# A streaming-encoder layer on one core: sigmoid's difference in one VectorE instruction, operand splits moved from GpSimd to VectorE, the final norm woven into later MLP pairs, and another place for the residual tile

## The chip, the core and the metric

The kernel runs on 1 core of one Trainium2 chip. The core has TensorE (PE in the profile; its weight loads are PEld), VectorE (DVE), ScalarE (ACT), GpSimd (POOL) and SyncE (SP, which here issues every DMA). The metric is the device time of one execution in microseconds (us); lower is better. The kernel before takes 3223.38 us, the median of 3 runs (3223.03 to 3224.46).

## The reference, cut to what matters

One layer with 1024 features over 2048 prompt rows and 32 sample rows: attention, an output projection, an MLP, a gate, a final norm. All is fp32. What the change touches begins after the attention:

```python
h = h + merge(oa, ob, ...)                       # [oa, ob] @ w_out
c = rmsnorm(h, g_mlp)
h = h + jnp.square(jax.nn.relu(c @ w_up)) @ w_down
h = h + jax.nn.sigmoid(h @ w_ple_gate) * (p @ w_ple_proj)
y = rmsnorm(h, g_final)
```

## The kernel before

The rows lie in four blocks: three of 512 rows and one of 544 (the last 512 prompt rows and the 32 sample rows). After the attention everything is kept transposed, features on the 128 partitions and rows along the free axis, so a block's residual `h` is a tile of 128 x 8 x 512 (or 544).

Every matmul is done three times to get fp32 precision (`mm3`, L215 to L217): both operands are split into a high and a low part, and high x high, high x low and low x high are added up in PSUM. So each operand costs a split: ScalarE copies the high part (L180), and the low part is a subtraction, on GpSimd through `pool_tt` (L165 and L175) or on VectorE (L186). Weights are split too, right after their DMA (`wunit`; tiles `wr` for the raw weight, `piece` for the parts).

`pool_tt` cuts an operation into equal instructions of at most `PW` = 256 columns: 512 columns are two of 256, 272 columns two of 136, 544 columns three of 181 or 182.

The last stage does, in this order of the program:

- `gate(1)` and `final(1)` for block 1; its residual lies in the pool `hq`, the split operands of its gate in `actq`, the output rows in `uq`.
- New pools are opened. `wp4` holds weights, `uh` (20 buffers) and `wk4` (among others 8 buffers `tmp`) the temporaries, and `hh` (2 buffers) the residual of the blocks still to come. Pools are stacked from the left and from the right end of SBUF; a tile that comes to lie on older tiles waits until those are no longer used. `hh` is opened on the left, so it lies where `actq` was.
- `outproj(2)` and `outproj(3)`, with `oload(3)` woven in: the output projections of blocks 2 and 3 (PSUM tile `ops`).
- `gate(0)`, woven with `cparts(2)`; then `mlp7(2)`; `gate(2)`, woven with `cparts(3)`; `mlp7(3)`; `gate(3)` and `final(3)`.

`gate(b)` computes, for each of 8 groups `d` of 128 features, the product `gps` = h @ w_ple_gate and `pps` = p @ w_ple_proj. Sigmoid comes as exp(min(z,0) - ln(1 + exp(-|z|))): ScalarE does Abs, Exp, Ln (L1236, L1238, L1239), VectorE min(z,0) from PSUM into `sm` (L1237), GpSimd the difference (`sig<-sm,sig`, L165), ScalarE Exp (L1245), VectorE the product with `pps` (L1259), GpSimd adds it to h (`h<-h,sig`). For the last two `d` of block 3 VectorE does both GpSimd steps.

`cparts(b)` prepares the up-projection's operands for `mlp7`, which replaces 8 block products by 7 (a Strassen-like scheme): for each of 4 steps `k` it loads two groups of h from DRAM, scales them (L976), forms sums (L988 to L991), and splits seven operands into `cs` tiles, four low parts on GpSimd and three on VectorE.

`mlp7(b)` runs over 16 pairs of feature blocks. Each pair loads and splits its weights (L1163 to L1166 form weight sums), does 7 up products (`ups`, combined at L1135), squares (L1139, L1140), splits, and lets the down products (`dps`, added to h at L1124) of the pair before run in between. `next(m)` issues one pair.

`final(b)` is, for each 128 rows: transposes on TensorE (`yp`, L1281), a copy to SBUF (L1289), a sum of squares on ScalarE (L1291), a small rsqrt, two scalings (L1310), and two DMAs out. Transposes use the PSUM pool `mm` with 2 banks; up products take turns over one ring of `mm` and twice `md` (6 banks). `weave(m, f, 1)` issues one step of `f` after each step of `m`.

The program's order is a priority only: a planner with its own cost model of the engines writes out each engine's queue from it, taking what is ready by that model. On the chip each queue then runs in that order; an instruction that waits holds up all behind it on its engine. That holds for SP's queue of DMAs too.

Of the kernel before, what the change touches and what calls it, by code (L numbers as in the profile page):

```python
# [12 lines left out]
F32 = mybir.dt.float32  # L13
F32R = mybir.dt.float32r
AF = mybir.ActivationFunctionType
ALU = mybir.AluOpType
# [3 lines left out]
P = 128  # L20
# [13 lines left out]
BLK = 544  # L34
# [42 lines left out]
JB = [(0, 1), (2, 3), (4, 5), (6, 7, 8)]  # L77
ONP = (28, 1, 6)
ONQ = (8, 1, 1)
PW = 256  # L80


def drain(gen):
    for _ in gen:
        pass
# [13 lines left out]
def weave(main, side, step, i=0, n=1):  # L99
    for _ in main:  # L100
        if i % step == 0:
            for _ in range(n):
                next(side, None)
        i += 1
    drain(side)
# [37 lines left out]
class Kern:  # L143
# [14 lines left out]
    def pool_tt(self, out, a, b, op):  # L158
        nc = self.nc
        if len(out.shape) == 2:  # L160
            n = out.shape[1]
            m = -(-n // PW)
            for i in range(m):
# [3 lines left out]
        k, n = out.shape[1:]  # L167
        if n > PW:
            for i in range(k):
                self.pool_tt(out[:, i], a[:, i], b[:, i], op)  # L170
            return
        s = PW // n
        for i in range(0, k, s):
# [789 lines left out]
    def cparts(self, b, wk, cs, out, r):  # L963
        nc = self.nc
        n, t0 = BN[b], 512 * b
        m = n // 2
        names = ("b11", "b21", "t2", "t1", "t3", "b22", "t4")
        ops = {x: [cs.tile([P, 4, 272], F32R, tag="cs", name="cs")[:, :, :m] for _ in range(2)] for x in names}
        out[b] = ops
        for k in range(4):  # L970
            c = []
            for i in range(2):
                tmp = wk.tile([P, BLK], F32, tag="tmp", bufs=self.nt, name="tmp")[:, :n]
                kk = k + 4 * i
                self.dma(tmp, self.hS[:, kk, t0 : t0 + n])
                nc.vector.scalar_tensor_tensor(  # L976
                    tmp, tmp, self.g_mlp[:, kk : kk + 1], r, op0=ALU.mult, op1=ALU.mult
                )
                c.append((tmp[:, :m], tmp[:, m:]))
            (b11, b12), (b21, b22) = c  # L980
            raw = {"b11": b11, "b21": b21, "b22": b22, "t3": b22, "t1": b12, "t2": b11, "t4": b21}

            def parts(*which):
                for x, e in which:
                    self.split(ops[x][0][:, k], ops[x][1][:, k], raw[x], "act", e)

            parts(("b11", "pool"), ("b21", "dve"), ("b22", "pool"))
            nc.vector.tensor_tensor(b22, b22, b12, op=ALU.subtract)  # L988
            nc.vector.tensor_tensor(b12, b12, b11, op=ALU.subtract)
            nc.vector.tensor_tensor(b11, b22, b11, op=ALU.add)  # L990
            nc.vector.tensor_tensor(b21, b21, b11, op=ALU.subtract)  # L991
            parts(("t2", "dve"), ("t1", "pool"), ("t3", "dve"), ("t4", "pool"))
            yield

    def colnorm(self, *args):
# [203 lines left out]
    def gate(self, b, h, up, act, md, wk=None):  # L1199
        nc, a = self.nc, self.a  # L1200
        n, t0 = BN[b], 512 * b
        Wg, Wp = a["w_ple_gate"][0], a["w_ple_proj"][0]
        pT = [[up.tile([P, BLK], F32R, tag="u", name="pT") for _ in range(2)] for _ in range(2)]
        for i in range(2):
            for k in range(2):
                self.dma(pT[i][k][:, :n], self.pS[:, i, k, t0 : t0 + n])
        if wk is None and act.aw is None:
            hc = [act.tile([P, 4, 272], F32R, tag="cs", name="hc").rearrange("p a b -> p (a b)") for _ in range(8)]
            hH, hL = [[hc[4 * i + k // 2][:, BLK * (k % 2) : BLK * (k % 2) + n] for k in range(8)] for i in range(2)]
        elif wk is None:  # L1210
            hH = act.tile([P, 8, act.aw], F32R, tag="act", name="hH")
            hL = act.tile([P, 8, act.aw], F32R, tag="act", name="hL")
            hH, hL = [[t[:, k, :n] for k in range(8)] for t in (hH, hL)]
        else:
            hH, hL = [[up.tile([P, BLK], F32R, tag="u", name="hu")[:, :n] for k in range(8)] for _ in range(2)]
        for k in range(8):
            self.split(hH[k], hL[k], h[:, k, :n], "act", "dve" if k % 2 else "pool")
        for dq in range(2):
            ph, pl = self.wunit(
                Wp[:, 512 * dq : 512 * dq + 512].rearrange("(k p) c -> p k c", p=P), [2, 512]  # L1220
            )
            for d4 in range(4):
                d = 4 * dq + d4
                wh, wl = self.wunit(Wg[:, P * d : P * d + P].rearrange("(k p) c -> p k c", p=P), [8, P])
                for s0, sn in SUBS[b]:
                    pg = md.tile([P, 512], F32, tag="mm", name="gps")[:, :sn]
                    self.mm3(
                        pg,
                        [(wh[:, k], wl[:, k], hH[k][:, s0 : s0 + sn], hL[k][:, s0 : s0 + sn]) for k in range(8)],
                    )  # L1230
                    sg, sm = [
                        (up.tile([P, BLK], F32, tag="u", name=x) if wk is None
                         else wk.tile([P, BLK], F32, tag="tmp", bufs=self.nt, name=x))[:, :sn]
                        for x in ("sig", "sm")
                    ]
                    nc.scalar.activation(sg, pg, AF.Abs)  # L1236
                    nc.vector.tensor_scalar(sm, pg, 0.0, None, op0=ALU.min)  # L1237
                    nc.scalar.activation(sg, sg, AF.Exp, scale=-1.0)  # L1238
                    nc.scalar.activation(sg, sg, AF.Ln, bias=1.0)  # L1239
                    end = b == 3 and d >= 6  # L1240
                    if end:
                        nc.vector.tensor_tensor(sg, sm, sg, op=ALU.subtract)
                    else:
                        self.pool_tt(sg, sm, sg, ALU.subtract)
                    nc.scalar.activation(sg, sg, AF.Exp)  # L1245
                    pq = md.tile([P, 512], F32, tag="mm", name="pps")[:, :sn]
                    self.mm3(
                        pq,
                        [
                            (  # L1250
                                ph[:, k, P * d4 : P * d4 + P],
                                pl[:, k, P * d4 : P * d4 + P],
                                pT[0][k][:, s0 : s0 + sn],
                                pT[1][k][:, s0 : s0 + sn],
                            )
                            for k in range(2)
                        ],
                    )
                    nc.vector.tensor_tensor(sg, sg, pq, op=ALU.mult)  # L1259
                    hv = h[:, d, s0 : s0 + sn]  # L1260
                    if end:
                        nc.vector.tensor_tensor(hv, hv, sg, op=ALU.add)
                    else:
                        self.pool_tt(hv, hv, sg, ALU.add)
                yield
# [64 lines left out]
    def run(self):  # L1330
        tc, nc, a = self.tc, self.nc, self.a
        with ExitStack() as top:

            def opened(stack, name, bufs, space=None, side="left"):
                kw = {} if space is None else {"space": space}
                return stack.enter_context(
                    tc.tile_pool(name=name, bufs=bufs, side=side, reuse_waits="tile", **kw)
                )
# [16 lines left out]
            sg = opened(s12, "sg", 2)  # L1355
# [26 lines left out]
            with ExitStack() as x:  # L1382
                wk = opened(x, "setup", 1, side="right")
# [6 lines left out]
            with ExitStack() as x:  # L1390
                pool = opened(x, "a0", 1, side="right")
# [44 lines left out]
            with ExitStack() as x:  # L1436
                pool = opened(x, "a1", 1, side="right")
# [3 lines left out]
            wk = opened(sq_, "wk", 1)  # L1441
# [15 lines left out]
            up = Sized(opened(top, "uh", 20, side="right"), BLK)  # L1457
# [8 lines left out]
            for b in HALVES[0]:  # L1466
# [5 lines left out]
                m = self.mlp((b,), {b: (h,) + cn[b]}, wk, uq, mm, mm)  # L1472
# [16 lines left out]
            wk = opened(top, "wk4", 1, side="right")  # L1489
# [1 line left out]
            self.nt = 8  # L1491
            self.rawp = Rings((self.wp, "wr"), (wk, "wr"))
            self.gfin(fk)
            hh = opened(top, "hh", 2)
            with ExitStack() as x:
                act = Sized(opened(x, "acth", 2), BLK, True)
                weave(self.outproj(2, wk, oa[2], md, acc[2]), self.oload(3, wk, act, oa), 1, 0, OW)
# [11 lines left out]
            f = self.final(0, h, up, fk, mm)  # L1509
            h = hload(hh, BLK, 2)  # L1510
            m = self.mlp7(2, h, ops[2], wk, up, mm, md)
            next(m)
            drain(f)
            drain(m)
            g = self.gate(2, h, up, None, md, wk)
            next(g)
            weave(g, self.cparts(3, wk, cs, ops, r3), 1)
            f = self.final(2, h, up, fk, mm)
            h = hload(hh, BLK, 3)
            m = self.mlp7(3, h, ops[3], wk, up, mm, md)  # L1520
            next(m)
            drain(f)
            drain(m)
            g = self.gate(3, h, up, cs, md)
            f = self.final(3, h, up, fk, mm, md)
            for _ in range(5):
# [48 lines left out]
```

## Time and profile before

| what | us |
|---|---|
| median of 3 runs | 3223.38 (3223.03 to 3224.46) |
| the profiled execution: time, span from first to last instruction | 3225.84, 3224.0 |
| PE busy in the span | 3036.1 (94%) |
| PEld, DVE, ACT, POOL busy | 2691.8, 1854.1, 1885.7, 1959.8 |
| mean granted TensorE clock | 0.976 of full speed |
| `gate(1)`'s last product to `outproj(2)`'s first | 2159.5 to 2169.7 |
| `gate(0)` with `cparts(2)`, start of `mlp7(2)` | about 2272 to 2400 |
| steady part of `mlp7(2)` | 2400 to 2690 |
| `gate(2)` with `cparts(3)`, start of `mlp7(3)` | about 2695 to 2840 |

The times in the table's lower half are us from the span's start. PE is the engine that is busy nearly always, so what matters is where it is not: in the second half of the span these are a few short places at the seams between the stages above. The profile tells for each how long PE was idle and what it waited for; the busy time of the others in the same stretch tells what was late.

### The profile page before, as it was taken

The numbers are of one execution on the slowest core, as the hardware profiler recorded it, in microseconds if no ns is written. First come the engines' busy times: TensorE is split into PE (matmuls) and PEld (weight loads), VectorE is DVE, ScalarE is ACT, GpSimd is POOL, SyncE is SP. The second block draws the span as 40 slices with busy tenths as digits, with TensorE's granted clock in tenths as the row PEclk, the third lists the DMA queues.
The fourth block names the chain that finished last, engine by engine and source line by source line (L and its number), as shares of the span: only waits on it lengthen the run. The fifth ranks groups of instructions, "written<-read, shape, count | busy, mean of one in ns | idle before, by whom it ended". The sixth has DMA issues, their size and how long they took to land.

```text
span 3224.0 us, 53645 instructions
## 1 busy us (share of the span) xinstructions
PE 3036.1 (94%) x18265; PEld 2691.8 (83%) x18265; DVE 1854.1 (58%) x4436; ACT 1885.7 (58%) x4166; POOL 1959.8 (61%) x2782
## 2 busy tenths in 40 slices
PE   8998989999999999999999999999989999799998
PEld 7787777899987787878788788878778898699998
DVE  5156774544465554676756656535676665766663
ACT  6256775766675664766666656444555545545455
POOL 4466556433345444665555545678977778877675
PEclk9998999999999999999999999999999999899999
DMA  8787768976787645555563543538443334233231
GB/s 264 244 246 216 202 193 249 252 222 194 216 247 218 193 131 140 160 153 140 162 187 114 142 117 106 175 114 247 119 139 99 99 104 127 80 104 96 92 116 55
DMA packets 512506, 521.63 MB, mean 162 GB/s; under 512 B 37948, under 2 KB 393600, under 8 KB 512232
## 3 DMA queue, kind: packets, MB, share of 16 engines
q1 hardware_dynamic: 512232, 518.19, 54.8%
q8 instruction: 145, 2.38, 0.3%
q14 instruction: 129, 1.06, 0.1%
HBM read 412.08 MB, written 109.95 MB: 162 GB/s over the span
## 4 chain that ended last, share of the span: by engine, by line
PE 53%; DMA 4%; DVE 4%; POOL 2%; ACT 2%; issue 1%; SPq 0%; DVEq 0%; ACTq 0%; POOLq 0%
PE dps L215 7%; PE dps L216 7%; PE dps L217 7%; PE ups L215 6%; PE ups L216 6%; PE ups L217 6%; PE s L632 2%; PE gps L216 1%; PE gps L215 1%; PE gps L217 1%; PE tpp L704 1%; DMA wr<-w_up 1%; DMA tmp<-hS 1%; POOL piece L175 1%; PE ops L215 1%
## 5 line engine op out<-in xcount | busy, mean ns | idle before, releaser
L175 POOL TENSOR_TENSOR wl<-wr,wh 128x256 fp32r<-128x256 f32 x648 | 473.7, 762 | 328.9 <-ACT wh L180 318.4
L180 ACT ACTIVATE piece<-wr 128x512 fp32r<-128x512 f32 x412 | 254.0, 627 | 310.8 <-PE ups L216 160.5
L175 POOL TENSOR_TENSOR piece<-wr,piece 128x256 fp32r<-128x256 f32 x416 | 334.3, 828 | 119.2 <-ACT piece L180 106.4
L180 ACT ACTIVATE wh<-wr 128x1024 fp32r<-128x1024 f32 x228 | 240.8, 1057 | 196.9 <-PE qps L216 52.2
L165 POOL TENSOR_TENSOR wl<-wr,wh 128x256 fp32r<-128x256 f32 x264 | 198.8, 783 | 182.1 <-ACT wh L180 176.8
L215 PE MATMUL ups<-cs,piece 128*128 128x256 f32 (+1 forms) x896 | 256.9, 287 | 10.3 <-ACT cs L180 5.4
L215 PE MATMUL dps<-uh,piece 128*128 128x272 f32 (+1 forms) x768 | 247.1, 327 | 16.0 <-ACT uh L180 15.6
L217 PE MATMUL ups<-cs,piece 128*128 128x256 f32 (+1 forms) x896 | 256.7, 287 | 0.6 <-POOL piece L175 0.6
L216 PE MATMUL ups<-cs,piece 128*128 128x256 f32 (+1 forms) x896 | 256.0, 286 | 0.5 <-DVE cs L186 0.5
L1124 DVE TENSOR_TENSOR h<-h,dps 128x272 f32<-128x272 f32 (+1 forms) x384 | 191.1, 514 | 100.3 <-PE dps L217 99.8
L216 PE MATMUL dps<-ul,piece 128*128 128x272 f32 (+1 forms) x768 | 247.9, 324 | 0.4 <-DVE ul L186 0.4
L217 PE MATMUL dps<-uh,piece 128*128 128x272 f32 (+1 forms) x768 | 247.2, 324 | 0.0
L215 PE MATMUL qps<-aH,wh 128*128 128x512 f32 (+1 forms) x640 | 230.2, 360 | 5.9 <-DVE ql L475 4.1
L165 POOL TENSOR_TENSOR piece<-wr,piece 128x256 fp32r<-128x256 f32 x280 | 223.1, 830 | 15.6 <-ACT piece L180 15.1
L215 PE MATMUL dps<-uh,wh 128*128 128x512 f32 x512 | 209.9, 410 | 21.3 <-ACT wh L180 7.4
L216 PE MATMUL qps<-aL,wh 128*128 128x512 f32 (+1 forms) x640 | 228.8, 357 | 0.0
L217 PE MATMUL qps<-aH,wl 128*128 128x512 f32 (+1 forms) x640 | 228.3, 357 | 0.0
L1083 DVE TENSOR_TENSOR h<-h,dps 128x512 f32<-128x512 f32 x256 | 174.2, 682 | 83.2 <-PE dps L217 78.5
L632 PE MATMUL s<-ka,q 128*128 128x512 f32 (+3 forms) x768 | 187.7, 347 | 22.5 <-DMA ka<-kS 12.1
L215 PE MATMUL ups<-cH,wh 128*128 128x512 f32 x512 | 202.7, 396 | 0.5 <-DVE h L1083 0.4
L216 PE MATMUL dps<-ul,wh 128*128 128x512 f32 x512 | 202.7, 396 | 0.0
L217 PE MATMUL dps<-uh,wl 128*128 128x512 f32 x512 | 202.3, 395 | 0.0
(300 smaller groups left out, 9839.0 us busy)
## 6 DMA issues: line engine op xcount, KB each, us to landing
wr<-w_up SPq DMA_DIRECT2D x128, 512.0 KB, 4.1
wr<-w_down SPq DMA_DIRECT2D x128, 512.0 KB, 3.7
wr<-w_in SPq DMA_DIRECT2D x74, 512.0 KB, 4.6
q<-qS SPq DMA_DIRECT2D x128, 256.0 KB, 5.3
v<-vSa SPq DMA_DIRECT2D x64, 512.0 KB, 3.7
ka<-kS SPq DMA_DIRECT2D x32, 512.0 KB, 7.9
wr<-w_out SPq DMA_DIRECT2D x32, 512.0 KB, 5.3
wr<-w_ple_gate SPq DMA_DIRECT2D x32, 512.0 KB, 4.1
```

What stands on the lines that cost most here:

```text
L165: nc.gpsimd.tensor_tensor(out[:, sl], a[:, sl], b[:, sl], op=op)
L175: nc.gpsimd.tensor_tensor(out[:, sl], a[:, sl], b[:, sl], op=op)
L180: nc.scalar.activation(hi, raw, AF.Copy)
L215: nc.tensor.matmul(ps, lh, rh, start=start and i == 0, stop=False)
L216: nc.tensor.matmul(ps, lh, rl, start=False, stop=False)
L217: nc.tensor.matmul(ps, ll, rh, start=False, stop=stop and i == n - 1)
L632: nc.tensor.matmul(s, q[:, m, hl, P * qi : P * qi + nr], kt[:, m, k0 - kb : k0 - kb + n], start=hl == 0, stop=hl == 1)
L704: nc.tensor.transpose(tp[:kn, x, :nr], w[:nr, P * i : P * i + kn], self.ident[:nr, :nr])
L1083: nc.vector.tensor_tensor(hv, hv, ps, op=ALU.add)
L1124: nc.vector.tensor_tensor(hv, hv, ps, op=ALU.add)
```

## The change

`PW` becomes 272. In `cparts` two of the four low parts move from GpSimd to VectorE. In `gate` one VectorE instruction, min(z,0) - sig, read from PSUM and SBUF, replaces VectorE's min and GpSimd's difference; it comes after Ln, and the tile `sm` is gone. `hh` is opened on the right side of SBUF. After `gate(0)` and `gate(2)` two MLP pairs are issued ahead of the final norm instead of one, and then one tile of 128 rows of it after each further pair instead of all four at once.

```diff
-PW = 256
+PW = 272
@@ cparts
-            parts(("b11", "pool"), ("b21", "dve"), ("b22", "pool"))
+            parts(("b11", "pool"), ("b21", "dve"), ("b22", "dve"))
...
-            parts(("t2", "dve"), ("t1", "pool"), ("t3", "dve"), ("t4", "pool"))
+            parts(("t2", "dve"), ("t1", "dve"), ("t3", "dve"), ("t4", "pool"))
@@ gate
-                    sg, sm = [
-                        (up.tile([P, BLK], F32, tag="u", name=x) if wk is None
-                         else wk.tile([P, BLK], F32, tag="tmp", bufs=self.nt, name=x))[:, :sn]
-                        for x in ("sig", "sm")
-                    ]
+                    sg = (
+                        up.tile([P, BLK], F32, tag="u", name="sig") if wk is None
+                        else wk.tile([P, BLK], F32, tag="tmp", bufs=self.nt, name="sig")
+                    )[:, :sn]
                     nc.scalar.activation(sg, pg, AF.Abs)
-                    nc.vector.tensor_scalar(sm, pg, 0.0, None, op0=ALU.min)
                     nc.scalar.activation(sg, sg, AF.Exp, scale=-1.0)
                     nc.scalar.activation(sg, sg, AF.Ln, bias=1.0)
                     end = b == 3 and d >= 6
-                    if end:
-                        nc.vector.tensor_tensor(sg, sm, sg, op=ALU.subtract)
-                    else:
-                        self.pool_tt(sg, sm, sg, ALU.subtract)
+                    nc.vector.scalar_tensor_tensor(sg, pg, 0.0, sg, op0=ALU.min, op1=ALU.subtract)
                     nc.scalar.activation(sg, sg, AF.Exp)
@@ run
-            hh = opened(top, "hh", 2)
+            hh = opened(top, "hh", 2, side="right")
...
             m = self.mlp7(2, h, ops[2], wk, up, mm, md)
-            next(m)
-            drain(f)
-            drain(m)
+            for _ in range(2):
+                next(m)
+            weave(m, f, 1)
...
             m = self.mlp7(3, h, ops[3], wk, up, mm, md)
-            next(m)
-            drain(f)
-            drain(m)
+            for _ in range(2):
+                next(m)
+            weave(m, f, 1)
```

## The prediction

> **What bounds the kernel now.** I read the page's busy shares and its 40 slices first, then the stages by windows, then what PE waited for in each, then what the other engines did there.
>
> ```profile
> span 3224.0 us, 53645 instructions
> ...
> PE 3036.1 (94%) x18265; PEld 2691.8 (83%) x18265; DVE 1854.1 (58%) x4436; ACT 1885.7 (58%) x4166; POOL 1959.8 (61%) x2782
> ...
> PE   8998989999999999999999999999989999799998
> ...
> POOL 4466556433345444665555545678977778877675
> PEclk9998999999999999999999999999999999899999
> ```
>
> PE is the bound almost everywhere: 94%. In the last third it dips in slices 27, 30 and 35, which are the seams that the change touches, and there POOL, not PE, stands at 7 to 9. The windows give the seams in us:
>
> ```profile
> core 0: us, PE busy (x) PEld busy (x) DVE busy (x) ACT busy (x) POOL busy (x), PEclk, DMA share, GB/s
> 2150.00:2180.00 30.00, 23.35 (x99) 18.44 (x98) 14.14 (x24) 14.22 (x35) 19.78 (x28) 0.83 0.53 165
> 2210.00:2240.00 30.00, 24.69 (x158) 22.09 (x157) 15.80 (x20) 16.17 (x30) 25.90 (x32) 1.00 0.79 243
> 2276.00:2360.00 84.00, 70.24 (x348) 58.22 (x347) 66.33 (x82) 50.65 (x105) 80.03 (x93) 0.95 0.30 89
> 2318.00:2345.00 27.00, 20.59 (x110) 17.24 (x109) 25.67 (x31) 15.93 (x34) 27.00 (x30) 0.94 0.13 34
> 2345.00:2372.00 27.00, 19.65 (x120) 17.66 (x118) 15.95 (x24) 13.12 (x29) 25.29 (x33) 0.81 0.35 114
> 2372.00:2400.00 28.00, 24.01 (x159) 21.17 (x158) 24.76 (x51) 14.56 (x38) 18.45 (x22) 1.00 0.65 231
> 2694.00:2792.00 98.00, 74.94 (x365) 62.50 (x364) 66.68 (x81) 51.18 (x103) 92.18 (x123) 0.89 0.31 91
> 2748.00:2770.00 22.00, 9.74 (x48) 7.95 (x47) 20.62 (x24) 11.61 (x25) 18.37 (x26) 0.69 0.15 47
> 2770.00:2795.00 25.00, 14.21 (x97) 13.76 (x98) 12.86 (x20) 11.77 (x24) 24.82 (x33) 0.80 0.28 86
> ```
>
> PE's idle time is the window less its busy time. Seam A (end of `gate(1)`): 6.65. Seam B (start of `outproj(3)`): 5.31. Seam C (`gate(0)` into `mlp7(2)`): 6.41 + 7.35 + 3.99 = 17.75. Seam D (`gate(2)` into `mlp7(3)`): 12.26 + 10.79 = 23.05. Together 52.8. On top, the granted clock is under 1 there; busy time times the missing share bounds that loss: A 23.35 x 0.17 = 4.0, C 20.59 x 0.06 + 19.65 x 0.19 = 5.0, D 9.74 x 0.31 + 14.21 x 0.20 = 5.9. It is an upper bound, since part of a slow period falls on idle time.
>
> What PE waited for in C, then in D:
>
> ```profile
> PE dps L215 <- ACT uh L180: 6.1, 1, 6.1
> PE pps L215 <- DVE sm L1237: 4.9, 1, 4.9
> ...
> PE dps L215 <- ACT uh L180: 9.5, 1, 9.5
> PE pps L215 <- DVE sm L1237: 6.9, 1, 6.9
> PE ups L215 <- ACT cs L180: 5.4, 1, 5.4
> ```
>
> `dps` waits for the first pair's operands, and these stand in DVE's and ACT's queues behind the gate's last groups, whose sigmoid goes through POOL. POOL has no slack: 80.03 of 84 in C, 92.18 of 98 in D. What it does there, C first, then D:
>
> ```profile
> L165 POOL TENSOR_TENSOR sig<-sm,sig 128x256 f32<-128x256 f32 x16 | 15.5, 987 | 1.6 <-issue 1.2 <-ACT sig L1239 0.4
> L165 POOL TENSOR_TENSOR cs<-tmp,cs 128x256 fp32r<-128x256 f32 x16 | 14.9, 944 | 0.0
> ...
> L165 POOL TENSOR_TENSOR cs<-tmp,cs 128x136 fp32r<-128x136 f32 x32 | 18.4, 601 | 3.6 <-ACT cs L180 3.6
> L165 POOL TENSOR_TENSOR h<-h,sig 128x256 f32<-128x256 f32 x16 | 14.4, 920 | 0.0
> L165 POOL TENSOR_TENSOR sig<-sm,sig 128x256 f32<-128x256 f32 x16 | 14.2, 908 | 0.0
> L165 POOL TENSOR_TENSOR piece<-wr,piece 128x256 fp32r<-128x256 f32 x9 | 6.3, 727 | 1.5 <-ACT piece L180 1.5
> ```
>
> **The change part by part.**
>
> *Sigmoid's difference.* It takes `sig<-sm,sig` off POOL: 15.5 us in C, 14.2 in D. On DVE one instruction replaces one:
>
> ```profile
> L1237 DVE TENSOR_SCALAR sm<-gps 128x512 f32<-128x512 f32 x8 | 5.4, 680 | 1.7 <-ACT sig L1236 1.7
> L1310 DVE SCALAR_TENSOR_TENSOR yo<-yp,rsy,gf 128x512 f32<-128x512 f32 x4 | 2.7, 745 | 0.1
> L186 DVE TENSOR_TENSOR cs<-tmp,cs 128x256 fp32r<-128x256 f32 x12 | 9.7, 818 | 0.0
> L186 DVE TENSOR_TENSOR cs<-tmp,cs 128x272 fp32r<-128x272 f32 x12 | 8.2, 682 | 0.5 <-ACT cs L180 0.5
> ```
>
> min takes 680 ns; the nearest row for the new form, a PSUM and an SBUF operand, is 745. So 0 to +0.07 a piece, 8 pieces a gate: under 0.6 us, on DVE. The new wait is for Ln: behind it in DVE's queue stand `cparts`' sums and the weight sums of the next pair, and the PSUM bank of `gps` is held past Exp and Ln, over which PE's `pps` waits. With 6 banks and two products a group the bank is wanted three groups on, and a gate's 8 groups fill 54 us of PE work, so some 20 us later; I take 0 for that; the bounds are -2 and +5 a gate, the upper one from the 4.9 that `pps` waits now. In return a `tmp` buffer less per group is asked for. At the program's end (`d` 6 and 7 of block 3) DVE did both steps already: 0.
>
> *Splits to DVE.* In C 8 of POOL's 16 go: -7.4. On DVE they cost 8 x 0.818 = 6.5, less if POOL leaves it alone. In D 32 POOL instructions of 136 columns become 8 of 272 (half are moved, the other half no longer cut). The price of 272 columns is not shown; from 256 undisturbed (727) to 256 disturbed (920) it would be 0.73 to 0.98 us scaled to 272; I take 0.9, as most here run disturbed: 7.2 instead of 18.4, so -11. DVE gets 8 x 0.682 = 5.5. So POOL falls by 23 to about 57 in C, by 25 to about 67 in D; DVE rises from 66.3 to about 72, from 66.7 to about 72. Both then lie at or under PE's own work in these windows (70.2 and 74.9). That is no longer POOL's bound, but DVE's slack is thin.
>
> The Trainium skill says against this move (Perfetto Trace Analysis, Optimizing Scalar/DVE Operations) that GpSimd and VectorE share an SBUF read port, so that offloading between the two might not help. By that rule the moved splits bring nothing (a rival below); the trace half agrees, as both are slower together, but a low part of 256 costs 944 ns on POOL and 818 on DVE in the same stage.
>
> *`PW` elsewhere.* Block 3's other operations of 272 and 544 columns need fewer POOL instructions; they lie under PE at 94%: 0.
>
> *Final norm spread.* The four tiles' DVE work no longer falls on the first pair; the 3.99 idle in 2372 to 2400 is its place in C. Afterwards 8 `yp` groups a block lie among full MLP pairs, where PE has no slack, in a ring with two banks. I take 1 us lost per block, 2 in all, bounds 0 to 20 (a rival below).
>
> *`hh` on the right.* This is seam A:
>
> ```profile
> SPq L156 <- PE gps L217: 19.3, 1, 19.3
> ...
> 2140.83 2.84 POOL L175 TENSOR_TENSOR wl<-wr,wh 128x256 fp32r<-128x256 f32 x4 [1.02 <-ACT wh L180]
> ...
> 2158.19 0.56 SPq L156 DMA_DIRECT2D h<-hS  x1
> 2158.87 15.45 SPq L156 DMA_DIRECT2D wr<-w_out  x4
> ...
> 2158.87 10.14 DMA wr<-w_out
> 2169.72 0.80 PE ops L215
> ```
>
> SP's queue stood 19.3 us at the load of block 0's `h`, since `hh` lies on `actq`, which `gate(1)` reads up to its last product. `w_out` stood behind it, though its raw buffer was last read by POOL at 2140.83 + 2.84 = 2143.7. It was issued at 2158.87, landed 10.14 later, and PE began at 2169.72. With `hh` elsewhere it can go out up to 14.5 us earlier and land before PE needs it. The load of `h` now waits for `final(1)` instead, as the new place (pool sizes added up from the right end) lies on `hq` and `uq`; it is first read when `gate(0)`'s split begins, in the midst of `outproj(2)`. I take 5 of 6.65, as the last `yp` groups still wait for the gate's last group. Seam B, fed by loads at one per step of `outproj(2)`, stays: 0, bounds 0 to 5.3.
>
> **The sum.** A 5. C: POOL's relief (23) exceeds the idle time (17.75), but DVE's queue order stays tight; I take two thirds, 12. D: two thirds of 23.05, 15. Clock, half of the bounds: 2 + 2.5 + 3 = 7.5. Less 2 for the final norm. 5 + 12 + 15 + 7.5 - 2 = 37.5. The profiled execution took 3225.84 (span 3224.0 and 1.84 around it), so 3188.3; it stands 0.08% above the median of 3223.38, so 3186.
>
> D holds one odd row:
>
> ```profile
> 2745.17 8.88 DVE L976 SCALAR_TENSOR_TENSOR tmp<-tmp,g_mlp_s,r 128x544 f32<-128x544 f32 x2 [3.73 <-DMA tmp<-hS]
> ```
>
> Two scalings took 8.88 us, and PE's waits for `cs` and `sm` (5.4 and 6.9) hang on them. POOL's row in the same stretch has no pause; I read it as DVE kept out until POOL pauses, which gets rarer with less POOL work. The Trainium skill (SBUF — State Buffer, SBUF: two separate sides) calls the shared port an exclusive lock held for the whole instruction; by that rule the wait would end with one POOL instruction, so the cause is another and may come back, and D would gain 8 less (sum 29.5).
>
> **The rivals.**
>
> *VectorE takes POOL's place.* The waits named after DVE stay: 4.9 and 3.99 in C, 6.9 in D; C gives 5, D 8, the clock 2.5, A 7 with its clock, less 2: 20.5, so 3203. For it: DVE is at 25.67 of 27 in 2318 to 2345, in order, and now also waits for Ln. Against: it is slow there because POOL runs beside it (818 ns for 256 columns).
>
> *Moved work is not freed work.* If POOL and DVE slow each other by as much as the moved splits take, only sigmoid's difference helps: of C's 12 the part 15.5 / 23, of D's 15 the part 14.2 / 25, so 8 + 8.5 instead of 27; the sum is 27, the time 3196. For it: low parts of 256 take 944 and 818 ns while both run. Against: the new sigmoid instruction reads PSUM and one SBUF operand, as `yo` does at an even 745. The Trainium skill's rule above is this rival.
>
> *The load of `h` in the new place stops SP.* If the planner puts it ahead of `w_out` again, it holds the queue until `final(1)` is done: A brings nothing (-7), and a second 10.14 us of starvation can follow: 37.5 - 7 - 10 = 20.5, also 3203. For it: that happened before. Against: what it waits for now ends later, so its turn should come later.
>
> *Slower: the final norm's transposes stall the MLP.* 16 `yp` groups go through the two-bank ring that up products also use; each bank is free only after DVE's copy and ACT's square. At 2.5 us a group it eats the 39.5 us gained elsewhere; at 4 us, 64 - 39.5 = +24.5, so 3248. For it: no slack in those pairs. Against: with eight groups in 2366 to 2400 PE lost at most 3.99, half a us each.
>
> *It does not do what it says:* PE's seams are set by the planned order, not by POOL; within 0.2%.
>
> **How the numbers follow.** The forecast case has 0.50 (its own range 3172 to 3201, from bounds of the seams), moved work 0.10, VectorE 0.16, SP 0.08, no effect 0.06, slower 0.10. Range 3168 to 3212: the low end is the seams without loss but B (3223 - 47.5 - 7.5), the high end takes in 3196 and both 3203 cases. About 0.2% is what a measurement of this kernel can tell from no change: faster 0.84, same 0.06, slower 0.10.
>
> **What would show it.** Right: POOL under 65 of 84 and 75 of 98 in the two hand-overs; no wait of SP for `gps` there, `ops` beginning within 3 us of the last `pps`; the clock at 1 in C. Wrong: `pps` waiting for the new DVE instruction; `yp` or `ups` waiting for DVE's copy or ACT's square inside `mlp7`; SP standing at `h<-hS`; new seams where the planner reorders.

## The result and the profile after

The changed kernel takes 3196.59 us (median of 4 runs, 3191.58 to 3199.06) against 3223.92 for the kernel before beside it (4 runs, 3223.03 to 3225.80): a ratio of 0.9913, 95% interval 0.9895 to 0.9930. The forecast was 3186 in a range of 3168 to 3212. The profiled execution took 3197.78, its span is 3196.0, that is 28.0 us shorter than before.

The page after, the same lines as before:

```profile
span 3196.0 us, 53414 instructions
...
PE 3037.6 (95%) x18265; PEld 2694.5 (84%) x18265; DVE 1851.6 (58%) x4448; ACT 1885.5 (59%) x4166; POOL 1887.4 (59%) x2572
...
PE   8998989999999998999999999998999999899998
...
POOL 4466546333335544565554555677787778867674
PEclk9998999999999999999999999999999999999999
```

PE's work is as large as before, so the 28 us are idle time and clock. GpSimd has lost 72 us, VectorE stands where it stood. The windows that the prediction used (busy us by engine, then clock):

```profile
2150.00:2180.00 30.00, 27.40 (x119) 21.72 (x118) 12.00 (x17) 13.64 (x30) 18.45 (x27) 0.94 0.33 94
2210.00:2240.00 30.00, 23.89 (x146) 22.50 (x145) 14.53 (x19) 13.49 (x25) 23.21 (x27) 0.84 0.80 264
2276.00:2360.00 84.00, 77.93 (x399) 66.06 (x398) 63.79 (x94) 52.79 (x110) 70.78 (x79) 0.96 0.32 101
2318.00:2345.00 27.00, 21.52 (x119) 18.90 (x118) 22.57 (x34) 17.61 (x36) 22.13 (x24) 0.87 0.17 59
2345.00:2372.00 27.00, 26.41 (x174) 23.85 (x173) 16.73 (x28) 15.95 (x30) 24.21 (x29) 1.00 0.34 98
...
2694.00:2792.00 98.00, 89.98 (x527) 80.19 (x526) 77.43 (x116) 59.64 (x118) 82.10 (x93) 0.95 0.33 104
```

Seams A, C and D are fuller. Seam B, 2210 to 2240, is worse: PE 0.8 us less busy, and the clock at 0.84 instead of 1.00. A window with fixed ends shifts against the stages, so lengths are better taken from the first product of each stage. In PE's timeline, before and then after (the row of `outproj(2)`'s first `ops` before stands in the prediction, 2169.72):

```profile
2159.14 0.39 PE L217 MATMUL pps<-pT,wl 128*128 128x512 f32 x1
...
2272.91 0.40 PE L215 MATMUL gps<-hu,piece 128*128 128x512 f32 x1
...
2695.13 0.39 PE L215 MATMUL gps<-hu,piece 128*128 128x512 f32 x1
...
3145.43 0.29 PE L215 MATMUL gps<-hc,piece 128*128 128x272 f32 x1
```

```profile
2160.83 0.40 PE L217 MATMUL pps<-pT,wl 128*128 128x512 f32 x1
...
2164.68 0.50 PE L215 MATMUL ops<-ou,piece 128*128 128x512 f32 x1 [1.77 <-ACT piece L180]
...
2272.70 0.40 PE L215 MATMUL gps<-hu,piece 128*128 128x512 f32 x1
...
2682.23 0.39 PE L215 MATMUL gps<-hu,piece 128*128 128x512 f32 x1
...
3117.29 0.29 PE L215 MATMUL gps<-hc,piece 128*128 128x272 f32 x1
```

From these: A is the time from `gate(1)`'s last `pps` to the first `ops`; "projections" runs from there to `gate(0)`'s first `gps`; C from there to `gate(2)`'s first; D from there to `gate(3)`'s first.

| stage, us | before | after | difference |
|---|---|---|---|
| up to `gate(1)`'s last product | 2159.5 | 2161.2 | +1.7 |
| A | 10.2 | 3.4 | -6.7 |
| projections | 103.2 | 108.0 | +4.8 |
| C | 422.2 | 409.5 | -12.7 |
| D | 450.3 | 435.1 | -15.2 |
| from `gate(3)` on | 78.6 | 78.7 | +0.1 |

They add up to -28.0. The windows of C and of D, cut at the same points, before and then after, show PE's idle time there: 17.75 and 23.88 us before, 8.08 and 9.70 after.

```profile
2272.91:2695.13 422.22, 404.47 (x2390) 356.16 (x2389) 285.56 (x436) 224.84 (x426) 334.19 (x414) 0.98 0.35 110
2695.13:3145.43 450.30, 426.42 (x3154) 413.57 (x3153) 300.33 (x558) 225.03 (x421) 349.03 (x484) 0.97 0.32 99
```

```profile
2272.70:2682.23 409.53, 401.45 (x2391) 353.84 (x2390) 281.34 (x444) 223.21 (x426) 322.77 (x389) 0.99 0.36 114
2682.23:3117.29 435.06, 425.36 (x3153) 412.83 (x3152) 300.94 (x566) 225.53 (x421) 320.13 (x395) 0.99 0.33 103
```

The waits of PE after, in the projections, in C, in D (`oact` is block 3's attention output, split for `outproj(3)`):

```profile
PE ops L215 <- ACT oact L180: 6.1, 2, 4.1
...
PE ups L217 <- POOL piece L175: 2.9, 1, 2.9
PE ups L215 <- ACT piece L180: 2.6, 1, 2.6
...
PE ups L215 <- ACT piece L180: 3.6, 1, 3.6
PE ups L217 <- POOL piece L175: 2.7, 1, 2.7
```

In C and D PE no longer waits for `sm`, and hardly for `uh`, the operand of the down products; what is late is the first MLP pair's weight pieces. What runs without a pause there is VectorE (windows of the kernel after, cut to its unbroken stretches; the fourth number is VectorE's busy time):

```profile
2284.78:2334.27 49.49, 48.68 (x227) 39.92 (x226) 47.84 (x71) 30.10 (x65) 40.06 (x41) 1.00 0.30 96
2697.90:2745.90 48.00, 45.36 (x210) 36.87 (x208) 47.52 (x65) 29.35 (x62) 38.32 (x40) 1.00 0.28 90
```

47.84 of 49.49 and 47.52 of 48.00: from the last steps of `colnorm`, which makes the row scale of the norm (in C), or `cparts`' first scaling (in D) to just ahead of the gate's last sigmoid products VectorE is full, while GpSimd is free for 9 us in each. That VectorE is full doesn't show yet that it ends the hand-over; two of the experiments bear on that.

### The profile page after: what moved, and what is told of

Its sections match the earlier page's. It is cut to its first block, busy times and chain, and to the rows that moved or that the text cites. A ratio compares the mean times of both kernels' runs of the same rounds, so it can differ in the third digit from the quotient of the medians.

```text
span 3196.0 us, 53414 instructions
## 1 busy us (share of the span) xinstructions
PE 3037.6 (95%) x18265; PEld 2694.5 (84%) x18265; DVE 1851.6 (58%) x4448; ACT 1885.5 (59%) x4166; POOL 1887.4 (59%) x2572
## 4 chain that ended last, share of the span: by engine, by line
PE 68%; DMA 12%; DVE 10%; ACT 4%; issue 3%; POOL 2%; SPq 1%; DVEq 0%; ACTq 0%; POOLq 0%
PE dps L215 6%; PE dps L216 6%; PE dps L217 6%; PE ups L215 6%; PE ups L216 6%; PE ups L217 6%; PE s L632 3%; PE qps L215 3%; PE qps L216 3%; PE qps L217 3%; DMA oraw<-oT 2%; PE ob L842 2%; PE tpb L817 1%; PE tpp L704 1%; DMA wr<-w_up 1%
## 5 line engine op out<-in xcount | busy, mean ns | idle before, releaser
L175 POOL TENSOR_TENSOR piece<-wr,piece 128x256 fp32r<-128x256 f32 x416 | 336.4, 834 | 103.2 <-ACT piece L180 87.8
```

The source lines that it names most:

```text
L175: nc.gpsimd.tensor_tensor(out[:, sl], a[:, sl], b[:, sl], op=op)
```

## The experiments

Three questions. Which part gave C and D their 28 us, and by which mechanism: GpSimd's load (the prediction's reading), or the round trip of sigmoid through GpSimd's queue? What made the projections longer: block 0's residual, which is now loaded among their own loads, or something else? And is what A gained still there at the end?

The stages of all kernels, from the first products as above, each from one profiled execution; "to `gate(2)`" is A, projections and C together. Kernels whose order differs little, such as the changed kernel and the one with 256 columns, differ by up to 3 us in a stage, so less than that is not read. The ratio is against the kernel before.

| kernel | A | proj. | C | D | to `gate(2)` | ratio, 95% interval |
|---|---|---|---|---|---|---|
| before | 10.2 | 103.2 | 422.2 | 450.3 | 535.6 | 1 |
| changed | 3.4 | 108.0 | 409.5 | 435.1 | 521.0 | 0.9913 (0.9895 to 0.9930) |
| sigmoid alone | 9.8 | 103.7 | 418.1 | 438.8 | 531.5 | 0.9944 (0.9929 to 0.9959) |
| splits alone | 9.9 | 103.7 | 427.2 | 443.3 | 540.8 | 0.9995 (0.9985 to 1.0005) |
| `hh` alone | 3.7 | 108.1 | 423.7 | 449.7 | 535.6 | 0.9997 (0.9986 to 1.0007) |
| spread norm alone | 10.1 | 104.4 | 418.3 | 453.8 | 532.7 | 0.9985 (0.9974 to 0.9995) |
| sigmoid, load kept | 10.0 | 102.8 | 421.6 | 448.2 | 534.4 | 0.9981 (0.9971 to 0.9991) |
| changed without splits | 3.4 | 106.0 | 412.2 | 434.5 | 521.6 | 0.9910 (0.9892 to 0.9928) |
| changed without spread norm | 3.4 | 108.8 | 416.9 | 434.7 | 529.1 | 0.9929 (0.9909 to 0.9949) |
| changed, load of `h` held | 3.4 | 103.4 | 416.9 | 435.0 | 523.7 | 0.9914 (0.9898 to 0.9929) |
| held, without splits | 3.5 | 103.2 | 416.4 | 435.9 | 523.1 | 0.9920 (0.9895 to 0.9946) |
| changed, 256 columns | 3.4 | 106.6 | 412.1 | 433.3 | 522.2 | 0.9908 (0.9890 to 0.9926) |
| changed, `oload` by twos | 2.6 | 105.9 | 411.3 | 435.9 | 519.8 | 0.9902 (0.9882 to 0.9922) |
| changed, `hh` on the left | 9.7 | 102.9 | 412.3 | 435.7 | 525.0 | 0.9920 (0.9903 to 0.9937) |

**Sigmoid alone.** The gate's edit of the diff on the kernel before.

> The kernel before with only the sigmoid edit (one VectorE instruction after Ln instead of VectorE's min and GpSimd's difference). Theory 1, GpSimd's work in the two hand-overs is what was late: it loses 15.5 of 80 us and 14.2 of 92 us there, 29.7 of the 48 us that the whole change takes off it, so about 17 us of the 28 us that seams C and D gained; the total near 3207. Theory 2, the round trip of sigmoid through GpSimd's queue is the whole cause (PE waited for uh, cs and sm behind it): 25 us or more, near 3198. Rival, VectorE takes GpSimd's place: under 8 us, and PE waits for the new VectorE instruction. Seams A and B keep their lengths (10.2 and 103.4 us from outproj(2)'s first to outproj(3)'s last product) within 1.5 us.

C and D fell by 4.2 and 11.5, 15.6 in all, and the medians by 18 to 21 us (0.9944): theory 1's number. But the number alone doesn't exclude a shorter queue path, so:

**Sigmoid, with GpSimd's load kept.** The new instruction, and a subtraction on GpSimd that nobody reads:

```diff
-                    nc.vector.tensor_scalar(sm, pg, 0.0, None, op0=ALU.min)
...
+                    if not end:
+                        nc.vector.tensor_scalar(sm[:, :1], pg[:, :1], 0.0, None, op0=ALU.min)
+                        hd = h[:, d, s0 : s0 + sn]
+                        self.pool_tt(sm, hd, hd, ALU.subtract)
+                    nc.vector.scalar_tensor_tensor(sg, pg, 0.0, sg, op0=ALU.min, op1=ALU.subtract)
```

> The sigmoid edit alone, but GpSimd keeps its work: per group it subtracts the residual from itself into sm, a tile that nobody reads (same sizes and count as sigmoid's difference before), and VectorE writes one column of sm first. So GpSimd's load, and the tmp buffer taken for sm, are as before, but sigmoid no longer goes through GpSimd's queue. Measured from gate(0)'s first product to gate(2)'s first (C) and from there to gate(3)'s first (D): before 422.2 and 450.3, sigmoid edit alone 418.1 and 438.8, together 15.6 us less. Theory 1, GpSimd's load was late: the 15.6 us go away, C and D together within 5 us of 872.5. Theory 2, the round trip of sigmoid through GpSimd's queue: they stay, together within 5 us of 856.8, and PE does not wait for sm.

C and D together took 869.8: 2.7 less than before, where the edit without the load gave 15.6. The medians give the load a smaller share: 0.9981 is some 6 us, 0.9944 is 18. The windows of the two hand-overs (sixth number: GpSimd), edit alone, then load kept:

```profile
2276.00:2360.00 84.00, 77.65 (x389) 65.44 (x388) 63.16 (x85) 52.12 (x108) 73.73 (x86) 0.96 0.32 99
2694.00:2792.00 98.00, 87.18 (x451) 74.83 (x450) 69.78 (x100) 55.80 (x119) 87.80 (x115) 0.93 0.33 103
```

```profile
2276.00:2360.00 84.00, 73.44 (x356) 61.16 (x356) 65.14 (x92) 50.83 (x107) 79.76 (x94) 0.92 0.28 86
2694.00:2792.00 98.00, 82.59 (x389) 68.71 (x388) 60.89 (x90) 52.13 (x108) 94.26 (x128) 0.90 0.30 92
```

The wait for `sm` goes with the round trip in both. With GpSimd at 79.76 and 94.26 again PE is idle for 10.56 of the 84 us and 15.41 of the 98; with the edit alone it is 6.35 and 10.82, before it was 13.76 and 23.06. So the shorter path does take idle time away, but with the load the clock stays at 0.92 and 0.90 (alone 0.96 and 0.93) and little of that is left in the time. In time GpSimd's work is the larger part, two thirds by the medians and more by the stages, and the shorter path the rest. The `tmp` buffer of `sm` came back together with the load; the two are not told apart.

**Splits alone**, with pieces of 256 columns:

> The kernel before with only the two low parts of cparts moved from GpSimd to VectorE (pieces of 256 columns as before). Theory 1, GpSimd's work is what was late: 7.4 us less in C and 9.2 us less in D, 16.6 of 48 us of relief, so about 10 us; near 3214. Theory 2 (sigmoid's round trip is the cause) and the rival that moved work is not freed work: within 3 us of before, as VectorE takes 12 us more in the two hand-overs while sigmoid's difference still stands in GpSimd's queue. Seams A and B unchanged.

No difference (0.9995): the second theory's and the rival's number. C came out 5.0 longer and D 7.0 shorter; why is not shown. **The changed kernel without them:**

> The changed kernel without the moved low parts (cparts gives four to GpSimd and three to VectorE again; 272 columns in one piece stay). Alone on the kernel before, the move gave 0.9995. If sigmoid carries the hand-overs and the splits bring nothing with it: C and D (409.5 and 435.1 us in the changed kernel) together within 4 us of 844.6, total within 4 us of the changed kernel. If the splits help only once sigmoid is off GpSimd (the parts alone gave 17 us, all together 30): 8 us or more longer, most of it as waits for weight pieces on GpSimd at the first MLP pair.

C and D together 846.7 against 844.6: no difference with sigmoid off GpSimd either. VectorE's row without a pause is shorter there, 41.2 and 42.8 us instead of 49.5 and 48.0, and GpSimd beside it is free for 3.4 and 1.3 us only:

```profile
2291.82:2333.06 41.24, 38.31 (x170) 31.05 (x170) 40.42 (x51) 24.59 (x54) 37.81 (x41) 0.96 0.24 77
2703.16:2745.95 42.79, 39.00 (x174) 31.72 (x173) 42.49 (x51) 25.41 (x55) 41.50 (x43) 0.96 0.25 76
```

So VectorE's row by itself is not what sets C and D. What GpSimd loses by the splits VectorE gets, and both ways the hand-over ends at the same time.

**`hh` alone:**

> The kernel before with only the residual's pool moved to the right side. If the load of block 0's h, which now goes out amid the loads of outproj(2), is what made outproj(2) and outproj(3) longer in the changed kernel: seam A is 6 to 7 us shorter (10.2 to 3.5), the two projections are 4 to 5 us longer (103.4 to 108), and C and D keep their lengths; total 2 us less than before, that is no difference. Rival, the 4.8 us come from another part of the change: A 6 to 7 us shorter with the projections as before, total 7 us less (3217).

As expected, 6.5 gained in A and 4.9 lost in the projections; nothing is left at `gate(2)` (535.6 both). So the loss in B belongs to this part. **The load of `h` held back** in the changed kernel:

```diff
-            h = hload(hh, BLK, 0)
+            h = hh.tile([P, 8, BLK], F32, tag="h", name="h")
+            nc.vector.tensor_copy(h[:, 0, 0:1], acc[2][0][:, 0:1])
+            self.dma(h[:, :, : BN[0]], self.hS[:, :, : BN[0]])
```

> The changed kernel, but block 0's residual is loaded only after outproj(2) is done: VectorE first writes one column of the new tile from outproj(2)'s sum of squares. Then no 2 MB transfer lies between the loads of block 3's attention output. If that load is what made the two projections longer (103.2 us before, 108.0 changed, 108.1 with the new place alone): 103 to 104.5 us, C, D and seam A unchanged, total 4 us under the changed kernel. Rival, the loads are late because the one-per-step schedule puts them late, whatever runs beside them: 107 to 109 us. Second rival, the load, now in outproj(3), delays outproj(3)'s or gate(0)'s own loads: 108 or more, with PE waiting for hd or piece there.

The mechanism first. In the changed kernel SP issues block 0's residual late in `outproj(2)`, between the loads of block 3's attention output (`oraw`, from which `oact` is made):

```profile
2207.75 0.57 SPq L156 DMA_DIRECT2D h<-hS  x1
...
2214.57 0.44 SPq L156 DMA_DIRECT2D oraw<-oT  x1
```

The DMA part of the profile gives the residual's size and its time to landing; behind it stands the time to landing of the `oraw` loads, as far as it is recorded (before, then after, then with the residual's load held):

```profile
h<-hS SPq DMA_DIRECT2D x2, 2048.0 KB, 9.3
```

```profile
DMA to landing us min/median/max: 3.1/3.1/3.6
```

```profile
DMA to landing us min/median/max: 3.0/3.9/6.2
```

```profile
DMA to landing us min/median/max: 3.1/4.3/6.0
```

The `oraw` issued behind the residual, at 2214.57, is the one that took 6.2. PE pauses 4.1 us for its `oact` and later 2.0 for another, and the clock is halved in the first pause and for some us behind it, and again 1 us after the second:

```profile
2220.30:2227.10 6.80, 4.66 (x20) 4.66 (x21) 5.45 (x8) 4.69 (x9) 6.80 (x7) 0.50 0.56 173
2237.40:2240.70 3.30, 3.30 (x15) 3.10 (x14) 2.41 (x6) 1.86 (x4) 1.40 (x3) 0.50 1.02 377
```

Half of 4.66 + 3.30 is 4.0 us; with 0.8 more of idle time that is the 4.8. With the load held the projections took 103.4, and the window 2210 to 2240 of that kernel shows the clock at 1.00:

```profile
2210.00:2240.00 30.00, 25.15 (x180) 23.58 (x179) 15.77 (x23) 13.64 (x24) 20.86 (x28) 1.00 0.67 216
```

So the loss in B goes with the moment at which the residual is loaded, and the schedule of one load per step is not its cause. The steps between are less plain: with the load held the `oraw` landed no sooner, and PE still waited 4.5 us for `oact` (6.1 changed, 4.0 before). But its longer pauses there were 1.9 and 2.6 us, in the kernel before 3.2, and behind none of these was the clock halved. All but 0.8 us of the loss is clock.

The total, however, did not move (0.9914), which I had not expected: C took 7.3 more. VectorE's stretch in that kernel:

```profile
2286.90:2335.80 48.90, 44.12 (x197) 35.30 (x195) 48.66 (x70) 27.06 (x59) 34.83 (x38) 0.96 0.26 85
```

As long as in the changed kernel, 48.66 of 48.90 busy, and begun later (125.9 us after `gate(1)`'s last product, there 123.6), though PE was at `gate(0)` 4.7 us sooner by the same measure: its first instruction, a scaling, waited for the `tmp` load. PE then waited 3.0 and 2.7 us for the first MLP weight pieces and 2.0 in the gate. Over the whole of C it was idle for 12.0 us (changed: 8.1) and busy 3.5 us longer with the same work, which is clock.

**Held, and without the splits:**

> The changed kernel with block 0's residual loaded only after outproj(2), and without the moved low parts. With the held load alone the projections took 103.4 us (108.0 changed), but C took 416.9 (409.5), so nothing was gained; VectorE ran there from 2286.9 to 2335.8 without a pause of over 0.5 us. If VectorE's row of work is now what ends the hand-over: about 6.5 us less of it lets C fall by 4 to 7 us, to 410 to 413, with the projections at 103 to 104, total 4 to 6 us under the changed kernel. Rival, GpSimd's chain ends it: C at 416 or more, total as the changed kernel or slower. Second rival, the order of the weight loads in SP's queue ends it: C within 1.5 us of 416.9.

C stayed (416.4): a miss. VectorE was not relieved in C: its low parts of 256 columns took 958 ns there instead of 791, beside a GpSimd that was busy 80.00 of the 90 us from 2275 to 2365 instead of 70.93. The numbers of both rivals came out, GpSimd's chain (416 or more, total as the changed kernel) and the order in SP's queue (within 1.5 of 416.9). PE's longest wait in C speaks for the first, but neither is shown:

```profile
PE gps L217 <- POOL piece L175: 7.0, 2, 6.2
```

**`oload` by twos** (the woven step count 1 becomes 2):

> The changed kernel with two steps of oload(3) after each step of outproj(2) instead of one, so that block 3's attention output is in before block 0's residual is loaded. If the transfers' meeting made the projections longer: 103 to 104.5 us instead of 108.0, PE's wait for oact at most 1 us. From the held load I expect that C takes part of it back: gate(1)'s last product to gate(2)'s first product 518 to 523 us (521.0 changed, 523.7 with the held load). Rival, C keeps its 409.5: 516 to 517 and 4 to 5 us less in all. Second rival, twice the splits of block 3's operands per step hold up outproj(2)'s weight pieces on ScalarE: outproj(2) longer than 49 us by 2 or more.

Between the forecasts. The wait for `oact` is gone, but a wait of 7.0 us for the high part of `colnorm`'s sums took its place, so the projections lost only 2.2. The kernel has the lowest median of all, 3195.18 (3192.42 to 3199.61); against the changed kernel's 3196.59 that is no difference.

**`hh` on the left again** in the changed kernel:

> The changed kernel with the residual's pool on the left again, as before. A is then about 10 us and the projections 103 to 104.5 (changed: 3.5 and 108.0). Theory, VectorE's row of work from cparts' first scaling to gate(0)'s last sigmoid (2284.8 to 2335.7 in the changed kernel, one pause of 0.9 us) ends the hand-over, and what PE gains or loses ahead of it is taken back in C: gate(1)'s last product to gate(2)'s first is 520 to 524 us (521.0 changed, 523.7 with the held load, 519.8 with loads two at a time), the total within 3 us of the changed kernel. Rival, seam A's 6.7 us are real at the end (the prediction's reading) and B's 4.8 are lost beside them: 2 us longer, 523 with C at 409.5. Second rival, the place of the residual is worth all of A: 527 or more, 6 us slower in all.

525.0 at `gate(2)`, 4.0 more than changed: between the two rivals, and above the theory's 524. Of A's 6.3 us B takes 5.1 back, so 1.2 of the 4.0 are left from these two; the other 2.8 lie in C, and so little is not read here. The ratios (0.9920 and 0.9913) don't tell the two kernels apart. So that the new place is worth something in this company is not shown, only that it is not worth A's 6.3.

**Pieces of 256 columns** in the changed kernel (`PW`):

> The changed kernel with GpSimd's pieces of at most 256 columns again, so that 272 columns are two instructions of 136. All other kernels with the sigmoid edit and 272 columns have D at 434.5 to 435.1 us, the sigmoid edit alone with 256 has 438.8 (32 pieces of 136 at 704 ns, 21.7 us). If the piece size carries that: D 437 to 440 with 16 pieces of 136, C within 2.5 us of 409.5. Rival, the 4 us come from the other parts: D within 1.5 us of 435.

D is 433.3: the rival is right, the piece size carries nothing. GpSimd's rows in D, changed, then with 256:

```profile
L165 POOL TENSOR_TENSOR cs<-tmp,cs 128x272 fp32r<-128x272 f32 x8 | 8.6, 1082 | 3.1 <-PE gps L217 1.9 <-ACT cs L180 1.2
```

```profile
L165 POOL TENSOR_TENSOR cs<-tmp,cs 128x136 fp32r<-128x136 f32 x16 | 13.7, 879 | 5.5 <-ACT cs L180 3.9 <-PE gps L216 1.5
```

5.1 us of GpSimd time are saved by not cutting, and D doesn't get shorter by it.

**The spread norm alone:**

> The kernel before with only the final norm spread over later MLP pairs. Theory of the prediction: the first pair of each of the two MLPs is relieved of the norm's VectorE and ScalarE work (up to 4 us of PE idle time in C, as much in D), and each later transposition costs little: 0 to 6 us faster, 3220. Rival, the transposes stall the full pairs in their two-bank ring: 4 us or more slower, with PE waits for VectorE's copy or ScalarE's square inside mlp7. Second rival, the norm's VectorE work was never what was late: within 1.5 us.

C 4.0 shorter, D 3.5 longer (it has the VectorE row of 6.59 us shown at the end), 0.9985. **The changed kernel without it:**

> The changed kernel without the spread final norm (four tiles of rows at once behind the first MLP pair, as before). From the spread norm alone (C 4.0 us shorter, D 3.5 longer, where a single VectorE addition lasted 6.59 us) I expect C 4 us longer than in the changed kernel (413.5) and D 0 to 3 us longer, total 4 to 7 us more. Rival, the norm's place matters more when the rest of the hand-over is tight: C and D together 9 us longer or more. Second rival, no effect: within 2 us.

C 7.4 longer, D the same, total 6 us more by the medians (the intervals of the ratios overlap, so this rests on C). In C the first pairs wait for the norm again:

```profile
PE ups L215 <- DVE r L1135: 2.7, 1, 2.7
PE yp L1276 <- ACT junk L1286: 2.6, 1, 2.6
```

So after sigmoid the spread norm is the second part that seems to pay.

## Why the prediction was right, point by point

Direction and range were right; the gain was 28.0 us from profile to profile, 37.5 forecast. The missing 9.5: B 4.8, D 1.8 and C 0.8 (each with a norm loss of 1 in the forecast), A 0.3, and 1.8 outside the change's stages, of which 1.7 were there before A began (that point lies anywhere from 2155 to 2166 us in the kernels run here).

By kind, from `gate(1)`'s last product to `gate(3)`'s first, PE's idle time fell from 53.6 to 26.5 us, 27.1 for a forecast of 30 (5 + 12 + 15 - 2). Its busy time, with the same work, fell by 2.7 for the 7.5 that were put down for the clock: by 3.0 in C and 1.1 in D, but over A and the projections it rose by 1.3. So the clock is the term that was mis-sized most, and B, where it stood at half twice, is where it went.

The rival "moved work is not freed work" gave 3196, within a microsecond of the measured median, and on the splits it was right. The number is luck all the same: it had C and D with their clock, less the norm, at 20 us, and they gave 27.9; B and the stretch ahead of A lost 6.5 that it did not have.

- **A: right.** 7 with the clock forecast, 6.7 measured; SP's wait of 19.3 for `gps` is gone. The `ops` began 3.4 us after the last `pps`, not "within 3". The page's PE row shows no dip in slice 27 (it has a 9 there); seam A is seen in the windows alone.
- **B: the step that failed.** The prediction put the load of `h` behind `final(1)` and gave B "0, bounds 0 to 5.3". It checked when the load is needed and what it waits for, not what 9.3 us of transfer do to the loads that PE waits for there. Measured: -4.8, outside the bounds, most of it clock. (The first read of `h`, 48.6 us after the first `ops` before, also lies where `outproj(2)` ends and not in its midst.) What A is worth was also taken as final; alone `hh` is worth nothing at `gate(2)`, in the changed kernel 4.0 at most.
- **Sigmoid on VectorE: right** in price, and in mechanism for the larger part: with GpSimd's load kept, 2.7 of the 15.6 us are left of the gain, by the medians 6 of the 18. The new instruction takes 680 to 682 ns against min's 680, and no `pps` waits for a bank:

```profile
L1239 DVE SCALAR_TENSOR_TENSOR sig<-gps,sig 128x512 f32<-128x512 f32 x8 | 5.5, 682 | 0.4 <-ACT sig L1237 0.4
```

- **Splits and `PW`: wrong as a source of gain.** They were to take 7.4 and 11 us off GpSimd and so a share of the 27; both were tested, and both gave nothing. GpSimd's low parts fell by 3.9 in C (14.9 to 11.0, since the 8 that are left took 1380 ns on average instead of 944) and by 9.8 in D; the 272 columns cost 1082, not 900 (and the forecast's lower bound, 727 ns scaled to 272 columns, is 0.77 and not 0.73). The 72 us forecast for VectorE in C do not lie "at or under" PE's own 70.2, as the prediction says. This is the rival "moved work is not freed work", right for the splits; sigmoid alone gave 15.6, about the 16.5 of its two shares there, but that is with its clock. The Trainium skill's sentence (Perfetto Trace Analysis, Optimizing Scalar/DVE Operations) that offloading between these two engines might not help agrees with both split experiments (0.9995 alone; 0.9910 without, 0.9913 with).
- **C and D: about right in size (12.7 for 13.5, 15.2 for 17), for partly other reasons.** GpSimd was to fall under 65 of 84 and 75 of 98; it stands at 70.78 and 82.10, since more of the MLP's own work now falls into these windows (its weight pieces took 43.3 us there instead of 37.9, and 52.7 instead of 40.0). The clock in C did not reach 1 throughout: it is 0.87 in 2318 to 2345 (0.94 before), but 1.00 in 2345 to 2372 (0.81 before). VectorE did take GpSimd's place as the engine without a pause, as that rival said; but without the splits its row is 8 and 5 us shorter and C and D are not, so it is not shown to end the hand-overs. What PE still waits for weight pieces is 5.5 and 6.3 us; its idle time was 17.75 and 23.88 before and is 8.08 and 9.70.
- **The odd row of D: not what made D long.** It did not come back. But `hh` alone has no such row either, its D is 449.7 (450.3 before), and PE waits 9.5 us for `sm` there: a long wait for `sm` needs no such row, and the 8 us that the prediction set on it are not borne out.
- **Final norm: half right.** The loss in later pairs is there, PE is busy 287.99 of 290 and 258.96 of 260 us in the steady parts (before 290.00 and 259.63), 2.0 and 0.7 us for a forecast of 1 each:

```profile
2400.00:2690.00 290.00, 287.99 (x1758) 255.41 (x1758) 190.78 (x305) 149.87 (x276) 225.22 (x278) 1.00 0.38 118
2840.00:3100.00 260.00, 258.96 (x2065) 258.70 (x2064) 170.73 (x346) 128.23 (x230) 181.59 (x231) 1.00 0.32 99
```

  But the relief of the first pair was put into C's relief by GpSimd, and it is a part of its own: 7.4 us in C.

What stays open: whether the hand-overs would end sooner if `cparts` began sooner. In D VectorE sits idle 12.43 us ahead of its row, until the first `tmp` lands; that was not tried.

```profile
2697.90 0.79 DVE L976 SCALAR_TENSOR_TENSOR tmp<-tmp,g_mlp_s,r 128x544 f32<-128x544 f32 x1 [12.43 <-DMA tmp<-hS]
```

## What to carry to other kernels

A transfer that is freed from one wait runs somewhere else: look up what else is in flight there, and price its duration against the loads that PE waits for, with the clock that a pause of some us can cost afterwards. Work taken off a full engine pays when it vanishes (two sigmoid steps became one) and not when it moves to the next fullest that slows down beside it. A gain at one seam is only worth what the next hand-over doesn't take back, so test a part with and without its company. Keep the load while taking away the wait to learn which of the two it was, and read idle time and clock apart when you do.

## What the hardware showed

Two VectorE instructions with two operands from SBUF lasted over many GpSimd instructions, until GpSimd made a pause. One is the odd row of the prediction, in the kernel before; the other, of 6.59 us, is in the kernel with the spread norm alone (VectorE, then GpSimd beside it):

```profile
2785.52 6.59 DVE L1163 TENSOR_TENSOR wr<-wr 128x512 f32<-128x512 f32 x1 [4.75 <-DMA wr<-w_up]
```

```profile
2786.08 2.07 POOL L165 TENSOR_TENSOR piece<-wr,piece 128x256 fp32r<-128x256 f32 x3
2788.12 1.39 POOL L165 TENSOR_TENSOR h<-h,sig 128x256 f32<-128x256 f32 x2
2789.49 2.07 POOL L165 TENSOR_TENSOR piece<-wr,piece 128x256 fp32r<-128x256 f32 x3
```

GpSimd's eight instructions end at 2791.56, VectorE's at 2792.11. The Trainium skill (SBUF — State Buffer, SBUF: two separate sides) has the loser wait for the whole of one instruction; here it waited for eight and more. In the 14 profiles no other VectorE instruction after 2150 us lasts over 2.5 us, so this is rare.
